# Softplus of the delta rule and of the state-space branch in short steps, and a longer price for VectorE's small operations on the program's clock

## The chip, the core and the metric

The kernel runs on one core of a Trainium2 chip. The metric is the time of one execution on the device in microseconds; from run to run it is given as a median. Its engines are TensorE (PE, with PEld its weight load), VectorE (DVE), ScalarE (ACT), GpSimd (POOL), and the queue SP, which here issues every transfer of weights.

## What is computed

Two blocks in a row, each of two layers, on 256 tokens of width 1024, in float32. The layers of the first block are called a0 and a1 here, those of the second b0 and b1.

```
a:  h = rms_norm(x); u = h @ w_in
    y = [mamba2(u), fox(u), moba(rope(u)), dsa(rope(u))]        # 4 branches of 512
    x += rms_norm((sum_n sigmoid(h @ w_gate + b_gate)_n * (y_n @ w_branch_n)) @ w_out)
    x += rms_norm(swiglu(rms_norm(x)))
b:  h = rmsnorm(x); z = h @ w_in
    o = [mla(z), spatial_gating(z), gla(z), deltanet(z)]        # 4 branches of 256
    x += (sum_n sigmoid(gates_n) * (o_n @ w_branch_n)) @ w_out
    x += cross_attention(rmsnorm(x), rmsnorm(mem));  x += squared_relu_mlp(rmsnorm(x))
out = rmsnorm(x)

mamba2:    dt = softplus(dt_raw + dt_bias)          # 8 heads; decay = exp(cumsum(-dt * exp(a_log)))
fox:       log_f = log_sigmoid(f_logit + f_bias)    # 8 heads
deltanet:  beta = sigmoid(bt);  qkv = silu(conv(q, k, v))
           g = -exp(a_log) * softplus(a + dt_bias)  # 4 heads; decay = exp(cumsum(g)) in chunks of 64
```

## The kernel before

Every product with a weight matrix is made of three matmuls, of hi and lo parts. A weight chunk arrives in a `raw` buffer by a transfer on SP; `high()` lets ScalarE write its hi part (`rt<-raw`, 128x1024 mostly), and `low()` lets VectorE write the lo part as the difference (`TENSOR_TENSOR rt<-raw,rt`). TensorE needs both, so a lo part that is late stops it. Names in the trace: `raw` raw weights, `rt` hi and lo parts, `ft` float32 working tiles, `bank` the PSUM banks, `qt` and `junk` other working tiles. All instructions are recorded by one helper, so their line is L364; a group is told by its tiles and shapes.

The order is made by a planner inside the program. `Model` keeps a clock for each engine; `Engine.call` (L363) records an instruction and adds the price that `Engine.cost` (L374) gives it. The matrix products are the spine. Between two groups of their matmuls `tick()` (L641) gives out everything else: branches are generators ("lanes"), and what stands between two `yield`s of one is a step, recorded in one piece. A lane is stepped when the time at which its last step ends on the program's clock has been reached by TensorE's clock, and when VectorE and ScalarE are not too far behind it (`behind()`); then `advance()` (L527) records hi and lo parts by their due times, which a first, dry pass of the same program has collected. On each engine the recorded order is the order of execution.

The softplus is `max(x, 0) + log1p(exp(-|x|))`; `softplus()` (L850) makes the absolute value and the exponential on ScalarE, `log1p()` (L831) a series on VectorE: a sum, a reciprocal, two products, a scaling, seven chained steps, a scaling and a last step. Its tiles have n elements in each of 128 partitions: n = 32 in `small()` (L1116) of the a layers (dt of the state-space branch and the log-sigmoid of fox in one), n = 8 in `dn()` (L2001) of the b layers, n = 256 in the gated linear attention `gla()`. For n over 64 the series has three pauses (`yield`), for the others none. `dn()` makes beta by a tanh on ScalarE and one VectorE operation, then the softplus, then the decays: a broadcast copy on GpSimd (`gx`) and small matmuls that read it.

Around `small()` in the a layers' heads lie the rotations of moba and dsa: products on VectorE (`ft<-bank,ft 128x512`), a sum on GpSimd (`ft<-ft 128x512`), transposes on TensorE. Around `dn()` in the b layers' heads lie the convolution of q, k, v by taps (products on ScalarE, sums on GpSimd), the latent attention (masks by `COPY_PREDICATED` on VectorE), the spatial gating and the gates `g` with the branch products `p`; the delta rule's branch comes last of the four.

Of the kernel before, what the change touches and what calls it, by code (L numbers as in the profile page):

```python
# [353 lines left out]
class Engine:  # L354
# [19 lines left out]
    def cost(self, fn, outs, ins, kw):  # L374
        if self.name == "PE":
            if fn == "transpose":
                return 109.0
            rows, m, n = ins[0].shape[0], ins[0].free_size(), ins[1].free_size()
            if ins[0].dtype == F32R:
                return max(m / 1.2, n / 2.4 + 12) + 1.5  # L380
            if rows <= 64 and m <= 64:
                return 68.0
            share = 0.67 if min(rows, m) <= 64 else 1.0
            return share * 2 * max(m / 1.2 + 1, n / 1.2 + 2)
        n = max(a.free_size() for a in outs[:1] + ins)
        psum = any("PSUM" in str(a.space) for a in ins + outs)
        ptr = sum(1 for a in ins if a.free_size() == 1) if n > 1 else 0
        if self.name == "ACT":
            return (94 if psum else 147) + n / 1.2 + 93 * (ptr + (len(outs) > 1))
        if self.name == "POOL":  # L390
            return 300 + 167 * n if kw.get("op") == OP.pow else 150 + 2.1 * n
        if fn in ("tensor_copy", "tensor_scalar", "memset") and not psum:
            return (n / 2 + 66) / 0.96 + 61 * ptr
        return (n + 66) / 0.96 + 61 * ptr + (1600 * n / 256 if fn == "reciprocal" else 0)


class Kern:
# [433 lines left out]
    def log1p(self, e, out, n):  # L831

        f = self.F.alloc(3 * n, "l1p")
        a, b, c = f.a[:, :n], f.a[:, n:2 * n], f.a[:, 2 * n:3 * n]
        self.ts(a, e, 2.0, OP.add)
        self.V.reciprocal(b, a)
        self.tt(a, e, b, OP.mult)
        if n > 64:
            yield
        self.tt(b, a, a, OP.mult)  # L840
        self.ts(c, b, 1.0 / 17, OP.mult)
        for k in (15, 13, 11, 9, 7, 5, 3):
            if n > 64 and k in (13, 7):
                yield
            self.stt(c, c, 1.0 / k, b, OP.add, OP.mult)
        self.ts(a, a, 2.0, OP.mult)
        self.stt(out, c, 1.0, a, OP.add, OP.mult)
        f.free()

    def softplus(self, x, out, n):  # L850
        f = self.F.alloc(2 * n, "sp")
        a, b = f.a[:, :n], f.a[:, n:2 * n]
        self.act(a, x, AF.Abs)
        self.act(a, a, AF.Exp, scale=-1.0)
        yield from self.log1p(a, b, n)
        self.stt(out, x, 0.0, b, OP.max, OP.add)
        f.free()
# [833 lines left out]
    def layer_b(self, l, hT, nxt, pr, early):  # L1691
# [309 lines left out]
        def dn():  # L2001
# [4 lines left out]
                yield  # L2006
            self.tt(v2(x4), tokv[:, :, 16:20], dtb[:, None, :].to_broadcast([128, 2, 4]), OP.add)
            self.act(v2(be), tokv[:, :, 20:24], AF.Tanh, scale=0.5)
            self.ts(be, be, 1.0, OP.add, 0.5, OP.mult)
            yield from self.softplus(x4, x4, 8)  # L2010
            self.act(ge[:, 0:4], alog, AF.Exp)
# [242 lines left out]
        for name in MORDER:  # L2254
            if name == "qk":
                convs("qk", 0, 2)
            elif name == "v":
                convs("v", 4, 1)
            elif name == "B":
                b = self.bank()  # L2260
                self.g2([b[:, 0:256], b[:, 256:512]], L, "B", hT, [(0, 128), (128, 256)], 4)
                self.act(gq.a, b[:, 0:256], AF.Copy, scale=32 ** -0.5)
                self.act(gk.a, b[:, 256:512])
                self.fbank(b)
                self.lane("C", gla())
            elif name == "E":
                self.block(L, "E", hT, 512, ev_E)
                self.lane("S", sgu())
            else:
                self.block(L, "dz", hT, 256, ev_dz)  # L2270
            placed.add(name)
            if name == "v":
                self.lane("B", dn())
# [470 lines left out]
```

## Time and profile before

| | |
|---|---|
| median of 3 runs | 2264.24 us (2263.59 to 2268.12) |
| the profiled execution | 2261.76 us |
| its span, first to last instruction | 2259.9 us |
| TensorE matmuls busy | 2220.2 us, 98% |
| VectorE busy | 1535.9 us, 68% |
| ScalarE busy | 1075.5 us, 48% |
| GpSimd busy | 300.4 us, 13% |
| mean granted clock of TensorE | 0.992 |

All times in the trace are counted from the span's start. The head of a0 is its first 50 us, that of a1 begins at about 560, that of b0 at about 1120, that of b1 at about 1700. A row of the timeline joins instructions of one kind that follow each other: its count is behind the x, the idle time of the engine just before it in brackets, with what released it. The stretches by window give the granted clock as PEclk: 1.00 is the full one.

### The profile page before, as it was taken

Reading aid. Unit: us, or ns where it says so; the run is one execution under the profiler, and the core shown is the slowest. Engines: PE = TensorE matmul, PEld = TensorE weight load, DVE = VectorE, ACT = ScalarE, POOL = GpSimd, SP = SyncE. Lnnn points to the kernel's source line nnn. Section 1 sums busy time; section 2 is a strip of 40 time slices with the busy share of each in tenths; the row PEclk is TensorE's granted clock in tenths of the full one; section 3 lists DMA queues with packets and bytes.
Section 4 is the critical chain, followed back from the end, with each engine's and each line's share of the span. In section 5 each row is a group of like instructions: output and inputs, shape, how many; then the busy total and the mean of one; then the engine's idle time right before and its main releaser. Section 6 shows DMA issues by size and latency. Waiting matters only on the chain.

```text
span 2259.9 us, 36096 instructions
## 1 busy us (share of the span) xinstructions
PE 2220.2 (98%) x14196; PEld 1898.7 (84%) x14196; DVE 1535.9 (68%) x2487; ACT 1075.5 (48%) x1699; POOL 300.4 (13%) x266
## 2 busy tenths in 40 slices
PE   8999999999999999999998999999999999999998
PEld 6887788999788788899886788988988677898897
DVE  7887777556888776764777767465566776746554
ACT  4555545444454554543554345444445533545543
POOL 2102110000302120000134220000002432000000
PEclk9999999999999999999998999999999899999999
DMA  6444665655444566565433265456553434544563
GB/s 220 150 133 144 202 227 183 209 176 174 149 131 141 163 202 219 202 215 187 151 105 122 95 206 182 142 176 230 181 163 113 139 112 161 187 159 158 188 210 106
DMA packets 108950, 379.37 MB, mean 168 GB/s; under 512 B 12730, under 2 KB 13164, under 8 KB 108780
## 3 DMA queue, kind: packets, MB, share of 16 engines
q1 hardware_dynamic: 108780, 377.07, 51.0%
q8 instruction: 111, 1.82, 0.3%
q14 instruction: 59, 0.48, 0.1%
HBM read 375.97 MB, written 1.05 MB: 167 GB/s over the span
## 4 chain that ended last, share of the span: by engine, by line
PE 87%; DVE 6%; POOL 2%; issue 2%; ACT 1%; DMA 1%; SPq 0%; POOLq 0%; DVEq 0%; ACTq 0%
PE bank L364 87%; DVE ft L364 4%; DVE rt L364 2%; POOL ft L364 2%; ACT ft L364 1%; DMA raw<-in_wts_a 1%; ACT rt L364 0%; DMA ft<-in_positions 0%; DMA raw<-in_wts_b 0%; ACT junk L364 0%; DVE qt L364 0%; ACT L364 0%; SPq L436 0%; POOLq L2739 0%; POOLq L364 0%
## 5 line engine op out<-in xcount | busy, mean ns | idle before, releaser
L364 PE MATMUL bank<-rt 128*128 128x512 f32 (+3 forms) x10608 | 1975.5, 344 | 13.4 <-DVE rt L364 12.3
L364 PEld LDWEIGHTS bank<-rt 128*128 128x128 f32 x10608 | 1647.7, 190 | 248.0 <-DVE rt L364 18.8
L364 DVE TENSOR_TENSOR rt<-raw,rt 128x1024 fp32r<-128x1024 f32 (+2 forms) x692 | 842.2, 1242 | 266.3 <-ACT rt L364 265.5
L364 ACT ACTIVATE rt<-raw 128x1024 fp32r<-128x1024 f32 (+2 forms) x692 | 693.9, 1034 | 302.1 <-PE bank L364 144.5
L364 POOL TENSOR_TENSOR ft<-ft 128x512 f32<-128x512 f32 (+9 forms) x208 | 247.4, 1200 | 1816.7 <-DVE ft L364 1673.7
L364 PE MATMUL bank<-ft 64*64 64x64 f32 (+13 forms) x3540 | 330.9, 268 | 19.5 <-DVE ft L364 11.8
L364 PEld LDWEIGHTS bank<-ft 64*64 64x64 f32 (+7 forms) x3540 | 254.4, 148 | 102.9 <-issue 35.3
L364 ACT ACTIVATE ft<-bank 128x512 f32<-128x512 f32 (+5 forms) x256 | 135.3, 537 | 334.6 <-PE bank L364 297.8
L364 ACT ACTIVATE ft<-ft 128x128 f32<-128x128 f32 (+7 forms) x238 | 107.6, 463 | 244.0 <-DVE ft L364 228.1
L364 ACT ACTIVATE rt<-bank 128x512 fp32r<-128x512 f32 (+1 forms) x114 | 63.3, 560 | 132.0 <-PE bank L364 131.7
L364 DVE TENSOR_TENSOR ft<-ft 128x512 f32<-128x512 f32 (+5 forms) x122 | 69.2, 568 | 74.2 <-ACT ft L364 71.9
L364 DVE SCALAR_TENSOR_TENSOR ft<-ft 128x512 f32<-128x512 f32 (+5 forms) x211 | 94.3, 467 | 35.1 <-ACT junk L364 16.2
L364 DVE TENSOR_TENSOR ft<-bank,ft 128x512 f32<-128x512 f32 (+8 forms) x160 | 74.1, 491 | 44.6 <-PE bank L364 31.0
L364 DVE SCALAR_TENSOR_TENSOR ft<-ft,bank 128x512 f32<-128x512 f32 (+1 forms) x110 | 70.8, 644 | 35.3 <-PE bank L364 25.7
L364 DVE TENSOR_TENSOR ft<-ft,bank 64x512 f32<-64x512 f32 (+3 forms) x88 | 56.6, 644 | 43.0 <-PE bank L364 39.8
L364 DVE SCALAR_TENSOR_TENSOR ft<-bank,ft 128x256 f32<-128x256 f32 (+5 forms) x124 | 60.4, 509 | 24.7 <-PE bank L364 9.3
L364 DVE TENSOR_SCALAR ft<-ft 128x256 f32<-128x256 f32 (+7 forms) x230 | 58.4, 297 | 26.0 <-ACT ft L364 10.4
L364 DVE COPY ft<-bank 128x384 f32<-128x384 f32 (+5 forms) x96 | 49.3, 541 | 28.5 <-PE bank L364 25.4
L364 ACT ACTIVATE junk<-ft 128x512 bf16<-128x512 f32 (+1 forms) x46 | 27.2, 592 | 64.4 <-DVE ft L364 61.6
L364 POOL TENSOR_SCALAR qt<-qt,ft 64x256 fp32r<-64x256 f32 (+1 forms) x32 | 37.2, 1164 | 131.5 <-PE bank L364 130.6
L364 DVE SCALAR_TENSOR_TENSOR rt<-bank,rt 128x512 fp32r<-128x512 f32 (+1 forms) x72 | 43.3, 612 | 16.5 <-ACT rt L364 16.2
L364 ACT ACTIVATE rt<-ft 128x512 fp32r<-128x512 f32 x46 | 29.0, 630 | 48.7 <-DVE ft L364 47.0
(37 smaller groups left out, 311.2 us busy)
## 6 DMA issues: line engine op xcount, KB each, us to landing
raw<-in_wts_a SPq DMA_DIRECT2D x340, 512.0 KB, 4.2
raw<-in_wts_b SPq DMA_DIRECT2D x312, 512.0 KB, 4.3
raw<-in_wts_b SPq DMA_DIRECT2D x24, 256.0 KB, 2.6
ft<-in_b_gate SPq DMA_DIRECT2D x16, 256.0 KB, 4.5
raw<-in_wts_b SPq DMA_DIRECT2D x8, 440.0 KB, 4.2
raw<-in_wts_a SPq DMA_DIRECT2D x8, 340.0 KB, 4.6
ft<-in_mem SPq DMA_DIRECT2D x4, 512.0 KB, 7.3
ft<-in_x SPq DMA_DIRECT2D x2, 512.0 KB, 3.7
```

The costliest lines, as they stand in the source:

```text
L364: r = None if self.dry else f(*args, **kw)
```

## The change

Three edits. In `Engine.cost`, VectorE operations of at most 64 elements in a partition, the reciprocal excepted, are priced at 185 ns plus 61 for each operand of one element; before, they went by their length, as (n + 66) / 0.96 or (n / 2 + 66) / 0.96 ns, 73 to 135 ns for these. In `log1p` the three pauses, and in `softplus` one after ScalarE's two operations, now hold for every n. In `dn()` a pause stands between the tanh of beta and the VectorE operation that reads it. No instruction is added or taken away; line numbers behind the first edit move by two or three.

```diff
--- before.py
+++ after.py
@@ -389,6 +389,8 @@
             return (94 if psum else 147) + n / 1.2 + 93 * (ptr + (len(outs) > 1))
         if self.name == "POOL":
             return 300 + 167 * n if kw.get("op") == OP.pow else 150 + 2.1 * n
+        if n <= 64 and fn != "reciprocal":
+            return 185.0 + 61 * ptr
         if fn in ("tensor_copy", "tensor_scalar", "memset") and not psum:
             return (n / 2 + 66) / 0.96 + 61 * ptr
         return (n + 66) / 0.96 + 61 * ptr + (1600 * n / 256 if fn == "reciprocal" else 0)
@@ -835,12 +837,11 @@
         self.ts(a, e, 2.0, OP.add)
         self.V.reciprocal(b, a)
         self.tt(a, e, b, OP.mult)
-        if n > 64:
-            yield
+        yield
         self.tt(b, a, a, OP.mult)
         self.ts(c, b, 1.0 / 17, OP.mult)
         for k in (15, 13, 11, 9, 7, 5, 3):
-            if n > 64 and k in (13, 7):
+            if k in (13, 7):
                 yield
             self.stt(c, c, 1.0 / k, b, OP.add, OP.mult)
         self.ts(a, a, 2.0, OP.mult)
@@ -852,6 +853,7 @@
         a, b = f.a[:, :n], f.a[:, n:2 * n]
         self.act(a, x, AF.Abs)
         self.act(a, a, AF.Exp, scale=-1.0)
+        yield
         yield from self.log1p(a, b, n)
         self.stt(out, x, 0.0, b, OP.max, OP.add)
         f.free()
@@ -2006,6 +2008,7 @@
                 yield
             self.tt(v2(x4), tokv[:, :, 16:20], dtb[:, None, :].to_broadcast([128, 2, 4]), OP.add)
             self.act(v2(be), tokv[:, :, 20:24], AF.Tanh, scale=0.5)
+            yield
             self.ts(be, be, 1.0, OP.add, 0.5, OP.mult)
             yield from self.softplus(x4, x4, 8)
             self.act(ge[:, 0:4], alog, AF.Exp)
```

Since the planner works with the prices and the steps, the order of the instructions moves in the heads of all four layers, the end of a1's feed-forward part and up to the gates of the b layers. Three places on VectorE follow; `TENSOR_TENSOR rt<-raw,rt` is a lo part of a weight, `128x32` and `128x8` the softplus.

VectorE, layer a1, around the softplus of `small()`; `ft<-bank,ft 128x512` are a rotation's products. Before:

```order
L364 TENSOR_SCALAR ft<-ft 128x2x8
L364 TENSOR_SCALAR ft<-ft 128x32
L364 RECIPROCAL ft<-ft 128x32
L364 TENSOR_TENSOR ft<-ft 128x32 x2
L364 TENSOR_SCALAR ft<-ft 128x32
L364 SCALAR_TENSOR_TENSOR ft<-ft 128x32 x7
L364 TENSOR_SCALAR ft<-ft 128x32
L364 SCALAR_TENSOR_TENSOR ft<-ft 128x32 x2
L364 COPY ft<-ft 128x16
L364 TENSOR_TENSOR ft<-bank_73,ft 128x512 x2
L364 TENSOR_TENSOR rt<-raw,rt 128x1024
```

Now:

```order
L364 TENSOR_SCALAR ft<-ft 128x2x8
L364 TENSOR_TENSOR rt<-raw,rt 128x1024
L364 TENSOR_TENSOR ft<-bank_72,ft 128x512 x2
L364 TENSOR_SCALAR ft<-ft 128x32
L364 RECIPROCAL ft<-ft 128x32
L364 TENSOR_TENSOR ft<-ft 128x32
L364 TENSOR_TENSOR rt<-raw,rt 128x1024
L364 TENSOR_TENSOR ft<-ft 128x32
L364 TENSOR_SCALAR ft<-ft 128x32
L364 SCALAR_TENSOR_TENSOR ft<-ft 128x32
L364 TENSOR_TENSOR rt<-raw,rt 128x1024
L364 SCALAR_TENSOR_TENSOR ft<-ft 128x32 x3
```

The products of the rotation stood behind the whole softplus, and no lo part within it; now they stand ahead of it, with lo parts between the softplus's pieces. In a0 the products move ahead of it likewise.

VectorE, layer b0, around the softplus of `dn()`; the first `TENSOR_SCALAR ft<-ft 128x8` is beta's. Before:

```order
L364 TENSOR_TENSOR rt<-raw,rt 128x512
L364 TENSOR_TENSOR ft<-ft 128x8
L364 TENSOR_SCALAR ft<-ft 128x8 x2
L364 RECIPROCAL ft<-ft 128x8
L364 TENSOR_TENSOR ft<-ft 128x8 x2
L364 TENSOR_SCALAR ft<-ft 128x8
L364 SCALAR_TENSOR_TENSOR ft<-ft 128x8 x7
L364 TENSOR_SCALAR ft<-ft 128x8
L364 SCALAR_TENSOR_TENSOR ft<-ft 128x8 x3
L364 TENSOR_TENSOR rt<-raw,rt 128x512
L364 TENSOR_TENSOR rt<-raw,rt 128x1024
```

Now (the `TENSOR_TENSOR ft<-ft 128x8` of the first step stands some rows further up):

```order
L364 TENSOR_TENSOR rt<-raw,rt 128x1024
L364 TENSOR_SCALAR ft<-ft 128x8
L364 TENSOR_TENSOR rt<-raw,rt 128x1024
L364 COPY_PREDICATED ft<-ft,bank_74 128x128
L364 COPY_PREDICATED ft<-ft,bank_75 128x128
L364 TENSOR_SCALAR ft<-ft 128x8
L364 RECIPROCAL ft<-ft 128x8
L364 TENSOR_TENSOR ft<-ft 128x8
L364 SCALAR_TENSOR_TENSOR ft<-ft,bank_72 128x256
L364 TENSOR_TENSOR rt<-raw,rt 128x1024
L364 COPY_PREDICATED ft<-ft,bank_71 128x128
L364 COPY_PREDICATED ft<-ft,bank_69 128x128
```

Beta's operation and the softplus stood in one piece between two lo parts; now lo parts, masks and a convolution's tap (`ft<-ft,bank 128x256`) stand between the pieces, of which the rows show the first two. The small matmuls that read the result stand some 100 matmuls later in TensorE's order than before.

VectorE, layer b1, the same step. Before:

```order
L364 TENSOR_TENSOR ft<-ft 128x8
L364 TENSOR_SCALAR ft<-ft 128x8 x2
L364 RECIPROCAL ft<-ft 128x8
L364 TENSOR_TENSOR ft<-ft 128x8 x2
L364 TENSOR_SCALAR ft<-ft 128x8
L364 SCALAR_TENSOR_TENSOR ft<-ft 128x8 x7
L364 TENSOR_SCALAR ft<-ft 128x8
L364 SCALAR_TENSOR_TENSOR ft<-ft 128x8 x3
L364 SCALAR_TENSOR_TENSOR ft<-ft,bank_69 128x256
L364 RECIPROCAL ft<-ft 128x4
L364 TENSOR_SCALAR ft<-ft 128x128
L364 TENSOR_SCALAR ft<-ft 128x256
```

Now:

```order
L364 TENSOR_SCALAR ft<-ft 128x8
L364 RECIPROCAL ft<-ft 128x8
L364 TENSOR_TENSOR ft<-ft 128x8
L364 SCALAR_TENSOR_TENSOR ft<-ft,bank_69 128x256
L364 TENSOR_TENSOR rt<-raw,rt 128x1024
L364 TENSOR_TENSOR ft<-ft 128x8
L364 TENSOR_SCALAR ft<-ft 128x8
L364 SCALAR_TENSOR_TENSOR ft<-ft 128x8
L364 COPY_PREDICATED ft<-ft,bank_74 128x128
L364 COPY_PREDICATED ft<-ft,bank_70 128x128
L364 TENSOR_TENSOR rt<-raw,rt 128x1024
L364 SCALAR_TENSOR_TENSOR ft<-ft 128x512
```

Behind the softplus stood the latent attention's reciprocal and scalings (`128x4`, `128x128`, `128x256`); now these are done further up, and lo parts, masks and taps stand between the pieces.

## Rows read from the trace of the kernel before

**Rows 1.** Page: busy us of TensorE; one group (busy us, mean ns | idle).
```profile
PE 2220.2 (98%) x14196; PEld 1898.7 (84%) x14196; DVE 1535.9 (68%) x2487; ACT 1075.5 (48%) x1699; POOL 300.4 (13%) x266
...
L364 DVE TENSOR_TENSOR rt<-raw,rt 128x1024 fp32r<-128x1024 f32 (+2 forms) x692 | 842.2, 1242 | 266.3 <-ACT rt L364 265.5
```

**Rows 2.** TensorE's waits by releaser (us in total, times, longest).
```profile
PE bank L364 <- DVE rt L364: 12.3, 12, 4.9
PE bank L364 <- DVE ft L364: 11.8, 6, 7.5
PE bank L364 <- POOL ft L364: 7.5, 9, 2.3
```

**Rows 3.** Windows (us; PE, PEld, DVE, ACT, POOL busy; PEclk, DMA, GB/s).
```profile
580.00:600.00 20.00, 17.44 (x82) 13.93 (x81) 17.98 (x45) 8.84 (x14) 8.09 (x8) 1.00 0.54 174
...
1190.57:1207.64 17.07, 12.81 (x79) 10.63 (x80) 10.03 (x25) 5.82 (x12) 6.59 (x5) 0.50 0.31 94
1774.25:1784.49 10.24, 10.24 (x52) 8.07 (x52) 6.03 (x15) 2.94 (x9) 1.33 (x3) 0.50 0.35 103
1791.31:1794.73 3.42, 3.42 (x27) 2.63 (x26) 3.42 (x6) 0.70 (x2) 1.90 (x2) 0.50 0.29 50
```

**Rows 4.** Timeline, b1's head, TensorE (start us, us, operation, count [idle before]).
```profile
1779.35 2.08 PE L364 MATMUL bank<-rt 128*128 128x512 f32 x4
...
1785.83 1.63 PE L364 MATMUL bank<-rt 128*128 128x512 f32 x6
```

**Rows 5.** Timeline, head of layer a0: TensorE and GpSimd.
```profile
23.50 0.33 PE L364 MATMUL bank<-ft 128*128 128x128 f32 x1 [0.74 <-POOL ft L364]
...
40.76 1.26 POOL L364 TENSOR_TENSOR ft<-ft 128x512 f32<-128x512 f32 x1 [6.26 <-DVE ft L364]
...
42.07 0.66 PE L364 MATMUL bank<-ft 128*128 128x128 f32 x4 [1.28 <-POOL ft L364]
```

**Rows 6.** Timeline, head of layer a1: the softplus's ends and what follows.
```profile
587.31 0.35 DVE L364 RECIPROCAL ft<-ft 128x32 f32<-128x32 f32 x1
...
590.50 0.17 DVE L364 COPY ft<-ft 128x16 f32<-128x16 f32 x1
...
591.94 2.17 POOL L364 TENSOR_TENSOR ft<-ft 128x512 f32<-128x512 f32 x1 [5.52 <-DVE ft L364]
...
594.17 0.66 PE L364 MATMUL bank<-ft 128*128 128x128 f32 x4 [2.28 <-POOL ft L364]
```

**Rows 7.** Timeline, head of layer b0: the softplus, and two waits of TensorE.
```profile
1187.35 1.31 DVE L364 TENSOR_SCALAR ft<-ft 128x8 f32<-128x8 f32 x2 [1.46 <-ACT ft L364]
...
1189.54 1.37 DVE L364 SCALAR_TENSOR_TENSOR ft<-ft 128x8 f32<-128x8 f32 x7
...
1191.58 2.23 DVE L364 TENSOR_TENSOR rt<-raw,rt 128x512 fp32r<-128x512 f32 x2
...
1192.32 0.80 PE L364 MATMUL bank<-rt 128*128 128x256 f32 x2 [4.91 <-DVE rt L364]
...
1200.16 0.18 ACT L364 ACTIVATE ft<-bank 128x8 f32<-128x8 f32 x1 [6.62 <-DVE ft L364]
...
1201.72 1.90 POOL L364 TENSOR_TENSOR ft<-ft 128x506 f32<-128x506 f32 x2 [6.96 <-ACT ft L364]
...
1204.38 0.69 PE L364 MATMUL bank<-ft 128*128 128x128 f32 x2 [2.51 <-DVE ft L364]
```

**Rows 8.** Timeline, head of layer b1: three waits of TensorE.
```profile
1771.15 0.30 PE L364 MATMUL bank<-ft 128*128 128x128 f32 x1 [0.86 <-DVE ft L364]
...
1771.81 0.44 PE L364 MATMUL bank<-ft 128*128 128x128 f32 x2 [0.36 <-DVE ft L364]
...
1791.01 0.99 PE L364 MATMUL bank<-rt 128*128 128x512 f32 x2 [2.01 <-DVE rt L364]
```

**Rows 9.** Timeline, heads of b0 and b1: two short waits of TensorE.
```profile
1214.08 0.48 PE L364 MATMUL bank<-ft 32*64 32x64 f32 x16 [0.70 <-POOL ft L364]
...
1763.59 1.66 PE L364 MATMUL bank<-rt 128*128 128x512 f32 x6 [0.78 <-DVE rt L364]
```

## The prediction

> **What bounds the kernel now.** I read the busy times first: TensorE's matmuls fill 98% of the span, 2220.2 of 2259.9 us [rows 1]. So a change that adds and removes no instruction can act in two ways only: on the time in which TensorE stands still, and on the pace at which it runs while it is busy. The list of TensorE's waits gives the first: 12.3 us for the lo parts of weights that VectorE makes, 11.8 us for other results of VectorE, 7.5 of them once at the start of the program, and 7.5 us for GpSimd [rows 2]. That leaves 12.3 + 4.3 + 7.5 = 24.1 us that a better order could remove in the whole kernel. The stretches by window give the second: at the head of layer b0 the granted clock is 0.50 for 17.07 us, at the head of layer b1 for 10.24 and again for 3.42 us [rows 3]; a stretch like 580 to 600, in layer a1, shows 1.00 [rows 3]. 0.50 is 1.2 GHz of the two levels, 1.2 and 2.4. What it costs is in the pace: six 128x512 matmuls took 1.63 us (0.27 each) at 1.00, four took 2.08 us (0.52 each) at 0.50 [rows 4]. So a half-clock stretch costs half of the time in which TensorE is busy in it: 12.81/2 = 6.4 us, 10.24/2 = 5.1 us and 3.42/2 = 1.7 us [rows 3].
>
> After that I looked at what stands ahead of the waits on VectorE. In all four layers' heads it is the same picture: 15 or 16 small operations of the log series of the softplus in one lump. Seven of them in a chain take 1.37 us on 128x8 [rows 7], 0.2 us each from start to start, and the page's time for a lo part is 1.24 us [rows 1], so a lump of 3.4 to 4.2 us is worth three lo parts, and VectorE takes its instructions in order.
>
> **The change, part by part.** *The price* (edit 1) executes nothing; it makes every small operation 185 ns long on the program's own clock. The traced 0.2 us of a dependent one is near that, so VectorE is now thought busy where it is, and steps are given out later. It reaches every small operation of the program, so everything after the first one is planned anew. *The pauses* (edits 2 and 3) cut the lump into four pieces on VectorE (five in the delta rule, where beta's operation is apart), between which the planner may put a lo part, a high part or another lane's step. What they cost in themselves is nothing: no instruction is added, and the reader of the softplus is pushed back too, as each head's account shows.
>
> Layer a0, −1.9 us. In the old order the products of the rotation stand behind the lump, GpSimd's sum behind them (40.76), and TensorE waits 1.28 us for that sum at 42.07 [rows 5]. In the new order these products stand ahead of the lump, at the same matmul as the lump stood before; GpSimd's sum of 1.26 us then begins some 3.4 us earlier while the transposes that read it come eight matmuls earlier (8 x 0.27 = 2.2 us, by the pace of rows 4), so 3.4 − 2.2 = 1.2 of the 1.28 us go. The 0.74 us at 23.50 [rows 5] is in front of transposes that now come six matmuls (1.6 us) later: gone. Together 1.9; bounds nothing, if GpSimd is late for another reason, and 1.28 + 0.74 = 2.0.
>
> Layer a1, −1.5 us. The lump goes from 587.31 to 590.67, the GpSimd sum of 2.17 us begins at 591.94, TensorE waits 2.28 us at 594.17 [rows 6]. In the new order one lo part (1.24 us) stands ahead of the products, and the lump behind: 3.4 − 1.2 = 2.2 us earlier. The transposes come six matmuls earlier, 1.6 us. GpSimd's sum took 2.17 us here and 1.26 us in a0 for the same shape; by the long one 2.28 − 2.2 + 1.6 leaves 1.7 us waiting, by the short one 0.8. I take the short one, since VectorE's small operations no longer run beside that sum: 2.28 − 0.8 = 1.5. Bounds 0 and 2.3.
>
> Layer b0, −13.8 us; the prediction hangs on this. VectorE stands 1.46 us for ScalarE's beta (tanh) [rows 7], with the whole softplus queued behind that wait; then the small operations run up to 1191.58, and only then comes the lo part for which TensorE has stood 4.91 us, at 1192.32. The half clock begins inside that standstill, 1190.57, and takes 6.4 us more. In the new order the tanh has a pause behind it, seven lo parts stand among the pieces, and the matmuls that read the decay (they need the end of the lump) come some 100 matmuls later than before. So the softplus ends in time: 7 x 1.24 = 8.7 us of lo parts on top, against 100 matmuls, 13 us even at half of 0.27 each. The third term is the 2.51 us at 1204.38: the last convolution's tap on GpSimd, 1201.72, was given out late because ScalarE stood for VectorE's copy [rows 7]; in the new order its last operation on VectorE precedes the transposes by 54 matmuls, 7 us at the same half. 4.91 + 6.4 + 2.51 = 13.8. Bounds: 7.4 if the half clock remains, 17 if the four smaller waits of this head go too (0.70 is one of them [rows 9]).
>
> By the Trainium skill ("TensorE: Matmul & The Clock Gate", section on HAM oscillation) the cost of a throttled stretch is half of its length. That would make the first stretch 17.07/2 = 8.5 us instead of 6.4; the trace shows 4.3 us of it without matmuls, which a slower clock can't lengthen, so the sum goes by the busy time.
>
> Layer b1, −4.9 us. 0.86 and 0.36 us at 1771 are the softmax scaling of the latent attention behind the lump; 2.01 us at 1791.01 is a lo part of the spatial gating's output, behind the delta rule's next operations on VectorE [rows 8]; in the new order the attention and the gating are through before that place, so 3.2 us go, and the second half-clock stretch, which begins at the 2.01 us, goes with its 1.7 us. The first one, 5.1 us, I leave standing: no long wait precedes it, so I can't name what would end it. Bounds 0 and 10.
>
> New waits, +5.9 us. A new plan never only removes: heads that are planned anew show waits of 0.70 and 0.78 us now [rows 9], and I put two such in each of the four: 4 x (0.70 + 0.78) = 5.9. Bounds 0 and 11.8.
>
> The sum: −1.9 − 1.5 − 13.8 − 4.9 + 5.9 = −16.2 us. The profiled execution took 2261.76 us, of which 1.86 lie outside the span, so 2245.6; the median of the runs is 2264.24, 2.5 us above it, and the same difference gives 2248.0.
>
> **Rivals.** *The half clock stays* (or comes back elsewhere). For it: at 1774.25 the clock fell with no long wait ahead of it, and at 594.17 it did not fall after 2.28 us, so the lump's long wait needn't be its cause. Against it: the two other stretches begin within a long wait. Then 6.4 and 1.7 us are not gained: −16.2 + 8.1 = −8.1 us, 2256.1. The Trainium skill has this as a second failure mode (same page, section on psum-queue depth-cycling): short idles between groups of matmuls let the clock swing. The stretch at 1774.25 agrees with it, the one at 1190.57 says nothing of it.
>
> *All goes right and more*: the stretch of 10.24 us at b1 ends too and no new waits come: −22.1 − 5.1 = −27.2, 2237.0. Against it speaks that every stretch of the old plan has its small waits.
>
> *Nothing arrives*: VectorE has as much to do in b0's head as before, and now the convolutions, the masking and the lo parts of the wide gates meet there, so a lo part is late all the same, behind another operation, and b0's 13.8 us return in part. With the a layers' 3.4 and half of the b layers' 18.7 us against the 5.9: −3.4 − 9.4 + 5.9 = −6.9, and without that half +2.5: within 4.5 us of 2264 for most of it. Against it: the new order shows lo parts between the pieces in all four heads, which the old one does not.
>
> *Slower*: in the new order the heads of b0 and b1 have the attention's masking copies (they read a score matmul's bank) between the pieces, with lo parts queued behind them. Where the matmul of the score is late, VectorE stands, and the lo part behind it is late as the one at 1192.32 was. One such place costs 4.91 + 6.4 = 11.3 us. One in each b head, 22.6 us, more than eats the gain: −16.2 + 22.6 = +6.4, 2270.6. It decides if both are late by about 5 us. Against it: of all the waits of the old plan only one is of that size, and one place alone still leaves −4.9.
>
> **How the numbers follow.** The forecast (−22 to −10) 0.52; more than that 0.11; the half clock stays (−10 to −4.5) 0.13; nothing arrives 0.12; slower 0.12. Differences under 0.2%, 4.5 us, are about what a measurement of this kernel can't tell from none. Faster is thus 0.52 + 0.11 + 0.13 = 0.76, same 0.12, slower 0.12. The range goes from the case of all right, 2237, to 2263, half of the nothing case; outside lie 0.12 slower, 0.06 of nothing and 0.02 of the better case: 0.20.
>
> **What would show it right or wrong.** Right: no wait over 2 us in b0's head, the reciprocal of 128x8 followed within some us by a lo part rather than by the rest of the chain, PEclk at 1.00 throughout b0's head, no wait for GpSimd at the first transposes of the rotation in a0 and a1. Wrong: a new TensorE wait for VectorE of 2 us or more in a b head, a masking copy with idle time before it, a half-clock window of 10 us or more that is new, or waits in the feed-forward and gate stages that the profile now shows clean.

## The result, and the profile after

The changed kernel takes 2239.35 us (median of 4 runs, 2239.25 to 2241.80) against 2263.91 us of the kernel before (4 runs, 2262.58 to 2268.12): ratio 0.9891, 95% interval 0.9874 to 0.9908, so 24.6 us less. The two profiled executions differ by 22.4 us, 2261.76 against 2239.36, and the accounts below are made of these. The forecast was 2248.0 us, in a range of 2237 to 2263.

The page and the list of TensorE's waits of the changed kernel, in the columns of [rows 1, 2]:

```profile
PE 2210.1 (99%) x14196; PEld 1893.2 (85%) x14196; DVE 1536.5 (69%) x2487; ACT 1075.3 (48%) x1699; POOL 289.9 (13%) x266
```

```profile
PE bank L364 <- DVE ft L364: 7.9, 3, 7.6
PE bank L364 <- POOL ft L364: 7.0, 10, 1.4
PE bank L364 <- ACT rt L364: 2.8, 4, 1.5
PE bank L364 <- DVE rt L364: 1.4, 4, 0.8
```

Two things moved. TensorE's waits for lo parts (`DVE rt`) went from 12.3 to 1.4 us, and its busy time from 2220.2 to 2210.1 us though it executes the same 14196 matmuls: 10.1 us of the gain is pace, and 22.3 − 10.1 = 12.2 us of the span's is standstill. The products with the weights come in one order in both kernels, so the time can be cut at the same matmuls. The windows that hold the same weights of the head of a0, the head and later part of a1 up to its feed-forward, the opening of b0, and the heads of b0 and b1 (length; PE, PEld, DVE, ACT, POOL busy; PEclk, DMA share, GB/s), of the kernel before:

```profile
0.00:422.67 422.67, 411.13 (x2277) 341.36 (x2278) 321.52 (x596) 211.48 (x353) 61.80 (x53) 1.00 0.55 182
578.20:916.93 338.73, 335.38 (x1838) 274.89 (x1837) 266.74 (x519) 169.99 (x296) 59.83 (x42) 1.00 0.54 168
916.93:1014.81 97.88, 96.15 (x617) 86.59 (x616) 63.74 (x100) 47.17 (x62) 1.10 (x2) 1.00 0.64 215
1153.56:1420.21 266.65, 256.20 (x2143) 213.95 (x2142) 195.24 (x331) 122.49 (x213) 74.00 (x64) 0.97 0.43 143
1728.80:2008.28 279.48, 274.32 (x2264) 228.27 (x2262) 196.85 (x337) 127.23 (x219) 70.29 (x64) 0.98 0.45 144
```

and of the changed kernel:

```profile
0.00:421.51 421.51, 410.96 (x2276) 342.06 (x2277) 320.57 (x596) 211.07 (x353) 64.23 (x53) 1.00 0.55 183
576.96:912.44 335.48, 334.90 (x1839) 274.90 (x1838) 266.33 (x520) 170.34 (x296) 51.66 (x42) 1.00 0.54 169
912.44:1014.85 102.41, 99.31 (x618) 89.25 (x617) 64.41 (x99) 46.94 (x61) 1.10 (x2) 0.97 0.62 209
1153.38:1408.63 255.25, 251.37 (x2143) 209.26 (x2142) 192.22 (x333) 122.17 (x213) 70.77 (x64) 1.00 0.45 149
1717.31:1985.83 268.52, 266.55 (x2264) 224.04 (x2263) 200.09 (x337) 128.36 (x222) 68.73 (x64) 1.00 0.47 149
```

The differences of the lengths are the accounts: a0 −1.2, a1 −3.3, the opening of b0 +4.5, b0's head −11.4, b1's head −11.0 us; the stretches between them differ by some 0.2 us or less. In b0's head 10.45 us without matmul became 3.88 and the mean clock went from 0.97 to 1.00; in b1's 5.16 became 1.97, and 0.98 became 1.00. b0's opening is the one place that lost: 1.73 became 3.10 us, and the mean clock fell there to 0.97, by a half-clock stretch of 6.83 us.

The head of b0 itself (timeline; start, length, operation, count, idle time before it in brackets), to be laid beside [rows 7]:

```profile
1189.85 0.48 DVE L364 TENSOR_SCALAR ft<-ft 128x8 f32<-128x8 f32 x1
...
1192.86 0.20 DVE L364 RECIPROCAL ft<-ft 128x8 f32<-128x8 f32 x1
...
1193.51 1.22 DVE L364 TENSOR_TENSOR rt<-raw,rt 128x1024 fp32r<-128x1024 f32 x1
...
1196.44 0.17 DVE L364 SCALAR_TENSOR_TENSOR ft<-ft 128x8 f32<-128x8 f32 x1
...
1196.85 1.22 DVE L364 TENSOR_TENSOR rt<-raw,rt 128x1024 fp32r<-128x1024 f32 x1
...
1200.01 1.63 DVE L364 SCALAR_TENSOR_TENSOR ft<-ft 128x8 f32<-128x8 f32 x4
...
1200.87 0.48 PE L364 MATMUL bank<-ft 32*64 32x64 f32 x16 [1.41 <-POOL ft L364]
```

Beta's operation starts without a wait for ScalarE (1.46 us before), lo parts stand between the reciprocal and the pieces of the chain, and the longest wait of TensorE in this head is 1.41 us, for GpSimd, where it was 4.91 for a lo part.

### The profile page after: what moved, and what is told of

Same layout as the page of the kernel before. It is cut to its first block, busy times and chain, and to the rows that moved or that the text cites. A ratio compares the mean times of both kernels' runs of the same rounds, so it can differ in the third digit from the quotient of the medians.

```text
span 2237.6 us, 36084 instructions
## 1 busy us (share of the span) xinstructions
PE 2210.1 (99%) x14196; PEld 1893.2 (85%) x14196; DVE 1536.5 (69%) x2487; ACT 1075.3 (48%) x1699; POOL 289.9 (13%) x266
## 3 DMA queue, kind: packets, MB, share of 16 engines
q8 instruction: 111, 1.82, 0.3%
## 4 chain that ended last, share of the span: by engine, by line
PE 87%; DVE 7%; ACT 2%; issue 2%; DMA 1%; POOL 1%; SPq 0%; POOLq 0%; DVEq 0%; ACTq 0%
PE bank L364 87%; DVE ft L364 5%; DVE rt L364 3%; POOL ft L364 1%; ACT rt L364 1%; DMA raw<-in_wts_a 1%; ACT ft L364 1%; DMA ft<-in_positions 0%; ACT junk L364 0%; SPq L438 0%; ACT L364 0%; DVE junk L364 0%; POOLq L2742 0%; DVEq L364 0%; ACTq L364 0%
## 5 line engine op out<-in xcount | busy, mean ns | idle before, releaser
L364 POOL TENSOR_TENSOR ft<-ft 128x512 f32<-128x512 f32 (+10 forms) x208 | 241.4, 1170 | 1807.5 <-DVE ft L364 1558.1
L364 PE MATMUL bank<-ft 64*64 64x64 f32 (+11 forms) x3540 | 322.0, 264 | 15.6 <-DVE ft L364 7.9
L364 PEld LDWEIGHTS bank<-ft 64*64 64x64 f32 (+7 forms) x3540 | 248.4, 145 | 95.4 <-issue 30.5
```

Of the source, the lines that this page charges most:

```text
L364: r = None if self.dry else f(*args, **kw)
```

## The experiments

The accounts under each kernel are made like those above, from the windows between the same weights. Each is of one profiled execution, with whatever clock that execution had, so the accounts need not add up to the difference of the medians.

### The price alone, the pauses alone

The first theory of the prediction was that the pauses bring the gain in place and the price only spreads the steps. The rival: the price alone makes the planner give lo parts out sooner. *The price alone* leaves the new price in `cost` and takes the pauses out:

```diff
+        if n <= 64 and fn != "reciprocal":
+            return 185.0 + 61 * ptr
```

> The kernel before with the longer price alone (edit 1); the softplus stays in one lump. Theory 1 (the pauses do it, because lo parts can stand between the pieces): the accounts of the b heads, -11.4 and -11.0 us in the changed kernel, do not come; 2255 to 2268 us, with a wait of 3 us or more for a lo part in b0's head and a half-clock stretch there. Theory 2 (the price does it, because the planner gives lo parts out sooner): 2238 to 2250 us.

2263.37 us (2262.22 to 2266.26), ratio 0.999 [0.998, 0.9999]: almost nothing, as the first theory had it. The lumps still stand whole, and TensorE still waits behind them in both b heads:

```profile
1192.35 0.51 PE L364 MATMUL bank<-rt 128*128 128x256 f32 x2 [4.47 <-DVE rt L364]
...
1759.58 1.37 DVE L364 SCALAR_TENSOR_TENSOR ft<-ft 128x8 f32<-128x8 f32 x7
...
1762.36 2.03 PE L364 MATMUL bank<-rt 128*128 128x256 f32 x10 [4.04 <-DVE rt L364]
```

The 4.91 us are 4.47, and b1 has a wait of 4.04 us that it had not before. Accounts: a0 −0.9, a1 −1.9, opening +4.6, b0 −3.5, b1 +3.4.

*The pauses alone* is the changed kernel without those two lines.

> The changed kernel with the old prices: the pauses alone (edits 2 and 3). Theory 1: 2238 to 2250 us, no half clock in either b head. Theory 2: 2255 to 2268 us. If each is worth about half, near 2252.

2273.00 us (2271.82 to 2279.30), ratio 1.0038 [1.0024, 1.0052]: slower than before, outside what either theory allowed. The profiled execution took 2278.14 us, 5 us above this median, and its accounts hold these too: a0 +2.4, a1 +2.5, opening +0.5, b0 +3.6, b1 +7.6. The lumps are gone, and other waits stand instead; GpSimd and TensorE in b0's head:

```profile
1181.51 0.51 PE L364 MATMUL bank<-rt 128*128 128x256 f32 x2 [2.12 <-DVE rt L364]
...
1261.69 3.91 POOL L364 TENSOR_TENSOR ft<-ft 128x128 f32<-128x128 f32 x4 [1.49 <-ACT ft L364]
...
1265.65 0.58 PE L364 MATMUL bank<-ft 64*64 64x64 f32 x3 [4.55 <-POOL ft L364]
```

The 2.12 us are a wait for a lo part that lies ahead of the softplus (its reciprocal comes at 1206); one of 1.54 us stood in the same stretch before, and with the price of 185 ns, alone or together with the pauses, TensorE waits there for no lo part over 0.3 us. The 4.55 us are the delta rule's own later part, behind four sums on GpSimd; b1 shows the same, 4.58 us. In the changed kernel the matmuls that answer to these wait 0.52 us in b0 and less than 0.3 us in b1. So pauses push the branch back, by 74 of the weights' matmuls (the first matmul that reads `gx` is preceded by 5788 of them before, 5862 with the pauses alone, 5854 with both), and what comes behind it must find room. Why the planner finds that room with the price and not without I can only argue: without it the clock holds VectorE to be free sooner than it is.

### Which pauses

With the price kept, the pauses were taken out by place. *Without those of the a layers* (the pauses under `if n != 32`), then *without those of the delta rule* (under `if n != 8`, and beta's out):

```diff
-        yield
+        if n != 32:      # the other kernel: n != 8
+            yield
```

> The changed kernel with the pauses left out for 32 elements (the a layers), kept for 8 (the b layers). If the heads are separate accounts: the a heads' -1.2 and -3.3 us are lost and the rest stays, so about 2244 us; the opening of b0 (+4.5 us in the changed kernel) shows whether it hangs on the a layers. If one head's order moves the next, any value from 2235 to 2260.

2241.33 us (2241.28 to 2244.38), ratio 0.9893 [0.9878, 0.9907], 2.0 us above the changed kernel. By the ratios (0.9893 against 0.9891) that is nothing these runs can tell.

> The changed kernel with the pauses in the a layers only; in the delta rule the softplus and beta are in one lump again, with the longer price. Theory 1: b0's and b1's gain (22.4 us) is lost, the a heads' 4.5 us stay, 2255 to 2265 us. Theory 2 (price): 2238 to 2250.

2252.85 us (2251.91 to 2254.34), ratio 0.9939 [0.9922, 0.9955], between the ranges of the two theories.

Without beta's pause alone:

```diff
             self.act(v2(be), tokv[:, :, 20:24], AF.Tanh, scale=0.5)
-            yield
```

> The changed kernel without the pause behind beta's tanh (edit 3). If VectorE's wait for ScalarE there (1.46 us before) is a part of the b heads' gain: 1 to 4 us slower, 2240 to 2244; if the pauses within the series are all: 2239.

2250.37 us (2247.97 to 2252.35), ratio 0.9935 [0.992, 0.995]: 11 us lost with one pause, nearly three times what I had expected at most. The whole set, accounts of the profiled executions in us, with the time that TensorE ran at half clock in the b heads (17.1 and 13.7 us in the kernel before):

| price | pauses a | pauses b | beta | a0 | a1 | opening | b0 | b1 | half b0 | half b1 | median |
|---|---|---|---|---|---|---|---|---|---|---|---|
| yes | – | – | – | −0.9 | −1.9 | +4.6 | −3.5 | +3.4 | 17.1 | 17.1 | 2263.37 |
| – | yes | yes | yes | +2.4 | +2.5 | +0.5 | +3.6 | +7.6 | 23.9 | 23.9 | 2273.00 |
| yes | – | yes | yes | −0.2 | −1.9 | +4.4 | −9.6 | −9.7 | 3.4 | 3.4 | 2241.33 |
| yes | yes | – | – | −1.2 | −3.2 | +3.6 | −8.3 | +1.8 | 3.4 | 23.9 | 2252.85 |
| yes | yes | yes | – | −1.1 | −3.3 | +4.6 | −5.1 | −5.8 | 13.7 | 3.4 | 2250.37 |
| yes | yes | yes | yes | −1.2 | −3.3 | +4.5 | −11.4 | −11.0 | 0 | 0 | 2239.35 |

b1's head needs the price and the pauses of the b layers together: without either it is longer than before. b0's head gains a part with the price and no pauses of its own. The price alone gives more than half of what a1 gains, and the loss at b0's opening comes with the price: all five kernels with it have it, the pauses alone do not. Row three has its waits in the b heads at the same matmuls as the changed kernel; its 1.8 and 1.3 us more there go with 3.4 us at half clock in each head. But the heads are not separate accounts throughout: row four differs from row one only in the a layers' pauses, and TensorE's longest wait in b0's head is 2.84 us there, for another result of VectorE, against 4.47 us for a lo part. Of the 4.8 us between the two accounts 0.7 are standstill; the rest goes with the shorter time at half clock.

The kernel without beta's pause shows in b1 what that pause does (timeline):

```profile
1755.25 1.24 DVE L364 TENSOR_SCALAR ft<-ft 128x8 f32<-128x8 f32 x1 [1.82 <-ACT ft L364]
...
1756.40 0.68 DVE L364 TENSOR_TENSOR rt<-raw,rt 128x512 fp32r<-128x512 f32 x1
...
1757.14 1.26 PE L364 MATMUL bank<-rt 128*128 128x256 f32 x6 [2.22 <-DVE rt L364]
```

VectorE stands 1.82 us for ScalarE's tanh, the lo part behind it is done at 1757.08, and TensorE has waited 2.22 us. In the changed kernel no wait of 1 us or more stands in b1's head. The b heads together stand still 3.2 us longer than in the changed kernel and b0's opening 1.2 us; most of the rest of the 11 us is pace, with TensorE busy 6.8 us longer for the same matmuls.

### Is the length of the lump the cause?

In the order of the kernel before, nine of the delta rule's sixteen operations are not executed in either b layer, while the planner still counts them (the softplus is thus another, and the result with it). The seven chained steps are shown; two more operations are left out in the same way:

```diff
+            self.model.mute = n == 8
             self.stt(c, c, 1.0 / k, b, OP.add, OP.mult)
+            self.model.mute = False
```

> The kernel before in its own order, with nine of the sixteen operations of the delta rule's softplus left out on VectorE in both b layers (the seven chained steps and two more; the decay is then another one): about 1.8 us less between beta and the next lo part. If the length of the lump is what keeps the lo part back: the 4.91 us wait at b0 falls to about 3.1, the 0.86 and 0.36 us at b1 vanish, and 3 us go in all, more if a half-clock stretch goes with them (up to 6.4 and 5.1 us). Rival, that the lo part waits for something else: nothing changes, 2264 us.

2258.15 us (2255.55 to 2263.38), ratio 0.9972 [0.9961, 0.9982]. The rows of b0, and the window of the half clock (columns as above):

```profile
1189.23 0.64 DVE L365 SCALAR_TENSOR_TENSOR ft<-ft 128x8 f32<-128x8 f32 x3
...
1189.79 2.23 DVE L365 TENSOR_TENSOR rt<-raw,rt 128x512 fp32r<-128x512 f32 x2
...
1190.53 0.71 PE L365 MATMUL bank<-rt 128*128 128x256 f32 x2 [3.08 <-DVE rt L365]
```

```profile
1190.70:1207.77 17.07, 14.56 (x87) 12.19 (x88) 10.30 (x20) 5.71 (x12) 7.48 (x7) 0.50 0.28 94
```

The lo part starts 1.79 us sooner, and the wait is 3.08 us instead of 4.91, as worked out: in b0 the lump's length is on TensorE's path one for one. At b1 the waits of 0.86 and 0.36 us are gone. But the half clock at b0 did not go with the part of the wait that went: it lies at the same place for the same 17.07 us, behind the 3.08 us that are left. The median fell by more than the 3 us of waits; the last section has a likely reason for that.

The other way round, *the changed kernel with 25 operations more* on VectorE behind beta's in b0, which the planner does not know:

```diff
             self.ts(be, be, 1.0, OP.add, 0.5, OP.mult)
+            for _ in range(25 if l == 0 and not self.V.dry else 0):
+                self.V.eng.tensor_scalar(out=be, in0=be, scalar1=1.0, scalar2=None, op0=OP.mult)
```

> The changed kernel with 25 more dependent operations of 128x8 on VectorE, some 5 us, behind beta's operation in layer b0, which the planner does not know of; the order is unchanged otherwise. If a late lo part stops TensorE and takes its clock as in the kernel before: a wait of 3 to 5 us there and a half-clock stretch, +5 to +11 us, 2244 to 2251. Rival, that the lo parts now stand far enough ahead: under 1.5 us, 2239 to 2241.

2248.44 us (2247.24 to 2251.29), 9 us above the changed kernel.

```profile
1190.10 6.17 DVE L2014 TENSOR_SCALAR ft<-ft 128x8 f32<-128x8 f32 x25
...
1197.46 1.67 PE L364 MATMUL bank<-rt 128*128 128x512 f32 x6 [0.98 <-DVE rt L364]
...
1198.73 2.71 POOL L364 TENSOR_TENSOR ft<-ft 128x256 f32<-128x256 f32 x2 [6.39 <-DVE ft L364]
...
1199.84 1.66 PE L364 MATMUL bank<-rt 128*128 128x512 f32 x6 [0.71 <-DVE rt L364]
...
1205.92 0.72 PE L364 MATMUL bank<-ft 32*64 32x64 f32 x16 [4.42 <-POOL ft L364]
```

The 25 take 6.17 us. TensorE waits 0.98 and 0.71 us for lo parts, and 4.42 us, where it was 1.41, for GpSimd, whose sums had stood 6.39 us for VectorE (0.88 us in the changed kernel). So of 6.2 us 4.7 reach TensorE, the larger part by way of GpSimd rather than by a lo part, and a half-clock stretch of 6.83 us comes with them, in this one execution. The new order has slack at this place, but little: about 1.5 us.

### The loss at b0's opening

Transfers are issued in order on SP. At b0's opening (timeline of SP, its line number by the kernel), before:

```profile
944.35 0.54 SPq L436 DMA_DIRECT2D ft<-in_pp  x1
953.92 0.33 SPq L436 DMA_DIRECT2D ft<-in_sgw  x1
...
955.71 13.46 SPq L436 DMA_DIRECT2D raw<-in_wts_a  x8
```

and in the changed kernel, with VectorE, ScalarE and TensorE:

```profile
936.46 0.78 SPq L438 DMA_DIRECT2D ft<-in_positions  x1
...
949.27 0.18 DVE L364 COPY ft<-ft 128x32 f32<-128x32 f32 x1
...
949.51 0.33 SPq L438 DMA_DIRECT2D ft<-in_norm_mix  x1
...
953.89 11.79 SPq L438 DMA_DIRECT2D raw<-in_wts_a  x8
...
959.06 1.06 ACT L364 ACTIVATE rt<-raw 128x1024 fp32r<-128x1024 f32 x1 [3.33 <-DMA raw<-in_wts_a]
...
960.17 12.06 PE L364 MATMUL bank<-rt 128*128 128x256 f32 x74 [1.48 <-ACT rt L364]
```

In both, one of the small parameters waits for its buffer, and those behind it, and then the weights, wait with it. Before, it was `sgw`, with three more behind it; now it is `norm_mix`, the first of them, which starts right behind VectorE's last copy out of the rotation table's workspace (949.27 and 0.18 us). So its buffer, as I read it, overlaps that workspace, freed in the plan but still in use. The weights start 1.8 us earlier than before, while TensorE is 4.5 us earlier; ScalarE then stands 3.33 us for a weight and TensorE 1.48 us for ScalarE. To test this against a plain lack of transfer speed, the workspace is freed only after the parameters have their buffers:

```diff
-        w.free()
+        st["pos"] = w
...
                 nxt_h["p"] = k.params(layers[i + 1])
+                if "pos" in st:
+                    st.pop("pos").free()
```

> The changed kernel with the workspace of the rotation table freed only after the small parameter transfers of layer b0 have their buffers, so that none of them waits on the queue for that workspace. If the blocked queue is what makes the weights late at b0's opening (TensorE waits 0.76 and 1.48 us, half clock for 6.83): -4 to -6 us, 2233 to 2236. Rival, the transfers themselves are too slow there: 2239. If the new plan moves the b heads as well, more or less than either.

2236.42 us (2235.15 to 2241.13), ratio 0.9878 [0.9863, 0.9893], just above the range that I had expected.

```profile
937.99 0.33 SPq L438 DMA_DIRECT2D ft<-in_norm_mix  x1
...
950.50 14.93 SPq L438 DMA_DIRECT2D raw<-in_wts_a  x9
...
957.49 0.97 PE L364 MATMUL bank<-rt 128*128 128x256 f32 x6 [0.76 <-DVE rt L364]
```

The parameters go out at once, the weights start 3.4 us earlier than in the changed kernel, TensorE's longest wait there is 0.76 us, and the account of the opening is −0.3 instead of +4.5. The two were run once more side by side:

> The kernel with the workspace freed late once more, beside the changed kernel on the same chip, for the difference of the two: 2.5 to 4.8 us faster than it (the account of b0's opening in the first profiles is +4.5 against -0.3 us, that of b1's head 0.9 us worse).

> The changed kernel once more, for comparison on the same chip: 2238 to 2242 us.

2238.42 us (2237.64 to 2243.19) against 2241.47 (2239.88 to 2243.91): 3.1 us, after 2.9 the first time. The opening gives its 4.6 to 4.8 us in both pairs of profiles. The medians show less. What can hide a part of it is seen in b0's head, in the windows between the same weights of two executions of the same kernel with the workspace freed late, in the first profile and in the second, whose execution was the slowest of its four:

```profile
1148.39:1403.71 255.32, 251.34 (x2143) 209.16 (x2142) 192.63 (x333) 122.19 (x213) 69.72 (x64) 1.00 0.44 149
```

```profile
1148.78:1411.09 262.31, 258.82 (x2144) 214.57 (x2142) 192.78 (x333) 122.31 (x213) 69.75 (x64) 0.97 0.45 145
```

The same instructions, 3.98 and 3.49 us without matmul, and 7.0 us apart: in the second, the clock was at half for 17.05 us. So a half-clock stretch is not always fixed by the program and its waits; this one came in one execution and not in the other. The two parts of it, 3.40 and 13.65 us by window, with TensorE busy throughout:

```profile
1205.00:1208.40 3.40, 3.40 (x12) 2.86 (x12) 0.82 (x3) 2.40 (x8) 0.87 (x2) 0.50 0.22 90
1232.30:1245.95 13.65, 13.65 (x102) 9.80 (x100) 7.35 (x15) 4.83 (x6) 1.28 (x1) 0.50 0.16 47
```

By the forecast's own reckoning that costs half of 17.05, 8.5 us; the two windows differ by 7.5 us in busy time and 7.0 in length. The Trainium skill ("TensorE: Matmul & The Clock Gate", section on HAM oscillation) also counts half of a throttled stretch as lost; the trace lies below that.

### Does the price have to be true?

The price of 185 ns is near what a dependent small operation takes (0.20 us from start to start in the chain of [rows 7]). With the workspace freed late, 130 and 250 were tried instead:

```diff
-            return 185.0 + 61 * ptr
+            return 130.0 + 61 * ptr      # the other kernel: 250.0
```

> The kernel with the workspace freed late, with 130 instead of 185 ns as the price. If the price has to be what the operations take (0.2 us from start to start in the trace): slower than 2236 by 5 us or more, towards the pauses alone (2273). Rival, that any price well above the old one does: within 3 us of 2236.

2244.17 us (2243.74 to 2244.78), ratio 0.991 [0.9893, 0.9926], 5.8 us above 185 on the same chip: b1's head loses 4 to 5 us, with 5.09 us without matmul instead of 1.3 to 2.0. The waits for lo parts ahead of the softplus stand at the same matmuls as with the pauses alone (1.57 and 1.42 us, there 2.12 and 2.11), while the two of 4.5 us at the delta rule's later part are gone.

> The kernel with the workspace freed late, with 250 ns as the price, longer than the trace shows. If the price has to be true: slower than 2236 by 3 us or more. Rival, that a longer price only pushes the steps further back and costs nothing: 2230 to 2237.

2234.77 us (2233.70 to 2236.75), ratio 0.9868 [0.9847, 0.9888], 3.7 us below 185 on the same chip and 6.7 below the changed kernel there. All four of its runs lie below the four of 185 on that chip, but not below all of the first four of 185. It is the fastest of the kernels here by its median. a1's head gains 4.6 and b0's 12.9 us; a0 stands 1.8 above the kernel before, with a half-clock stretch of 3.41 us there. So the price need not be true, as the rival had it. The longest is the best of the three here, whether by a rule or by the chance of one plan is not told by three points.

## Why the prediction was right, and where it was not

**The direction and the place** were right: the two b heads hold the gain, in b0 the lump of the softplus ahead of a lo part was the cause (the wait shrinks one for one when the lump does), and no wait above 2 us is left there. Of the 24.6 us, though, 16.2 were forecast. The sum held 8.1 us of standstill (14.0 us of waits gone, 5.9 new) and 8.1 us of clock; the two profiles differ by 12.2 us of standstill and 10.1 of busy time. The largest difference lies in one head.

**b1's head, −4.9 forecast (−3.4 with its share of new waits), −11.0 measured.** The three waits named are gone, and the head stands still 3.2 us less (5.16 − 1.97), as much as they were. That the numbers agree is in part luck: waits of 0.52, 0.78 and 0.37 us went that the sum left out, and 0.43 and 0.88 us came. The step that failed is "The first one, 5.1 us, I leave standing". Both half-clock stretches of [rows 3] were gone, 13.65 us of half clock, and TensorE's busy time in the head fell by 7.8 us where 1.7 were forecast. What the runs show in its place: this head ran 0 to 3.4 us at half clock in all nine profiles of kernels with a longer price and with the pauses of the delta rule's series, and 13.7 to 23.9 us in the five others. So the stretch went with the order, though no long wait precedes it. What in the order keeps the clock up there stays open.

**b0's head, −13.8 forecast (−12.3 with its share of new waits), −11.4 measured.** The waits of 4.91 and 2.51 us went, and with them 1.54, 0.70 and 0.57 us; new ones of 0.64, 1.16, 1.41 and 0.52 us came, all for GpSimd. In all 6.6 us of standstill are gone. The term for the clock was too large: 6.4 us, while the busy time fell by 4.8 us, though the whole stretch was gone. Its reason, that the half clock belongs to the 4.91 us standstill, was neither refuted nor shown: the stretch stayed for 17.07 us when that wait was cut to 3.08. It came without such a wait too, in one of two executions of the kernel with the workspace freed late, whose longest wait in this head is 1.42 us. "The half clock stays" was a rival with the right doubt. One of the two stretches that its answer puts within a long wait, the one at 1791.31, begins 0.3 us behind it [rows 3, 8].

**The a layers, −1.9 and −1.5 forecast, −1.2 and −3.3 measured.** The waits of 1.28 and 2.28 us are gone whole: the transposes that answer to them, at 37.80 and 589.17, wait for nothing. Wrong in a0: the 0.74 us at 23.50 did not vanish, it is 0.65 at 24.99, and the other one of 0.74, at 34.55, which the sum left out, went; a new wait of 0.59 stands at 53.38. In a1 the term left 0.8 of the 2.28 us standing, and it had nothing for the 0.71 us at 604.05, which is 0.41 us now (at 595.27). GpSimd's sum took 1.29 us (at 587.83), the short value, but not for the reason given: in the old order the softplus had ended at 590.67, before that sum began, and in the new one two of its operations run beside it.

**New waits, +5.9 forecast, spread over four heads.** In the heads 0.59 us came in a0, 3.7 in b0 and 1.3 in b1, 5.6 us in all; but 4.5 us of small old waits, which the sum let stand, went from the two b heads, so the size is luck. And the sum had no term for b0's opening, +4.5. The place is a queue that the change moves nothing on: SP's, held by a buffer that the new plan gave to another transfer.

**The parts of the change.** "The price executes nothing" and the pauses as the working part were half of it: the pauses alone cost 7.6 us, the price alone gives 2.1, both 24.6. The forecast took the joint effect from the new order, and so did not depend on this; its reasons did. Beta's pause, which I had costed within b0 only, is worth 11 us.

**The price of a half-clock stretch**, half of the busy time in it, was too high where two executions of one kernel could be laid beside each other (8.5 against 7.0 to 7.5 us). Against the change of TensorE's busy time in whole heads it was too high in b0 (6.4 against 4.8) and too low in b1 (half of 13.65 is 6.8, against 7.8). What decided more was how often the clock fell.

## What to carry to other kernels

Where a planner orders in-order engines, a long step of small operations is a wait for whoever stands behind it; cut it, and price it as long as it takes or longer: here each without the other gave almost nothing or lost. After each new plan look at the queues that nobody touched: a freed buffer given to the next transfer cost 4.5 us. And before a clock term goes into a sum, look at the clock in several executions, not at one trace.

## What the runs showed of the hardware

The granted clock makes the spread of the runs. 33 executions of the kernel before have mean clocks from 0.988 to 0.993 and times from 2261.37 (0.993) to 2270.68 us (0.989), the slower at the lower clock almost throughout; 8 of the changed kernel have 0.996 to 0.998. From 0.989 to 0.993 the mean time falls by some 6 us, 1.5 us for 0.001; the median clock went from 0.991 to 0.997, so I estimate that about 9 us of the 24.6 are clock, near the 10.1 us of busy time that the two profiles differ by. This would also explain the median of the kernel with nine operations left out: its profile, at a mean clock of 0.990, took 2263.38 us, and the runs next to its median are at 0.992 and 0.994.

At b0's opening a wait of 1.48 us (1.56 in the second profile) stands beside a half-clock stretch of 6.83 us in both profiles of the changed kernel, while 2.28 us at 594.17 brought none [rows 3, 6]. Over all fourteen profiles TensorE has 24 waits of 2 us or more behind the first 10 us. In 20 of them, the nine longest (3.08 to 5.75 us) among these, a half-clock stretch begins within the wait or at most 2.1 us behind its end; two lie within a stretch that had begun before, and two, both at 594 in a1, have none. Stretches began without such a wait too, as at 1774.25 [rows 3]. So a long wait mostly had the half clock with it, and what decides in the other places was not settled.
